# The opening of a one-core decoder step: dt in four column groups, smaller first pieces, half the zeros, and unit 2's casts in the hand-written list

## The chip, the cores and the metric

The kernel runs on one core of one Trainium2 chip. The metric is the time of one execution on the device in microseconds (us); lower is better. Engines are named as in the profile: PE (TensorE, matmul), PEld (its weight loads), DVE (VectorE), ACT (ScalarE), POOL (GpSimd) and SP (SyncE, which issues most transfers).

## The reference

One layer of a hybrid decoder for 256 prompt tokens and 8 single sample tokens, all in float32. What the change touches is its beginning: the RMSNorm and the input projection, of which dt is the last 32 columns.

```python
def rms_norm(x, g):
    xf = x.astype(jnp.float32)
    y = xf * lax.rsqrt(jnp.mean(xf * xf, axis=-1, keepdims=True) + EPS)
    return (y * g.astype(jnp.float32)).astype(x.dtype)
...
    proj = rms_norm(x, w['g_mix']) @ w['w_in']
    q, k, v, z, xbc, dt_raw = jnp.split(proj, IN_SPLITS, axis=-1)
...
    dt = jax.nn.softplus(dt_raw.astype(jnp.float32) + dt_bias.astype(jnp.float32))
```

After it come sliding-window attention, the state-space scan, an output projection, cross-attention and a convolutional feed-forward part, each with a residual. The change leaves them as they are.

## The kernel before

The tokens of both groups lie side by side as 264 columns; features lie on partitions, so x is 16 blocks `k` of 128x264 (`xT`, four tiles of four blocks). Nearly all products are float32 in three steps (`mm3`, L97 to L100): an operand is split into a rounded part `hi` in the format fp32r and a remainder `lo`, and hi·hi + hi·lo + lo·hi is accumulated. ScalarE makes `hi` (a cast of weights, or a scaling of x by the gain), VectorE makes `lo` (a subtraction).

Weights come in *units* of 8 blocks x 256 columns (128x2048), each as two *parts* of 128x1024; a part is loaded into `wraw` and split into `whi` and `wlo`. Each of these tiles has four buffers (`WBUFS`), taken in turn: the cast of part n must wait until TensorE has read part n-4. Units 0 and 1 (parts 1 to 4) give the first 256 columns of the projection, units 2 and 3 (parts 5 to 8) the next 256, unit 4 begins the third 256. The normalisation is applied at the end: r0 = 1/rms is computed beside the products, and every result is multiplied by r0 as it leaves its PSUM bank. PSUM banks go by tags: `mm` has three, `t` two, `x` and `y` one each. dt holds one `mm` bank, units 2 and 3 the two others; unit 4 takes the bank of dt when that has been evacuated.

The opening (L183 to L243) is a list written out by hand, in which SP, PE, ACT and DVE keep the order of the code. In it:

- eight F32 products of zeros (`warm`, L187) run ahead of the first data;
- x comes in pieces of two blocks (`load_x`), unit 0 in four pieces of 512 columns (`w_load`); the splits of x (`x_hi` L147, `x_lo` L151) alternate with those of the weights;
- the dt weights (128x512 for all 16 blocks) are split as well, and dt is computed in three steps per block (`dt_k`, 48 products of 32x264 through `mm3`): eight blocks between units 0 and 1, eight behind unit 1.

Behind the list a scheduler orders the work by simulated times. The norm's four squares (L305, ScalarE, each over one `xT` tile) and their sum (L306 to L309, VectorE) are held back by `issue_after`, which sets an edge from each instruction of the block to a named one *on the same engine*: here the last split of x on ScalarE and on VectorE. The sum is added over partitions by a product with ones (`total`, L274, F32), then ScalarE takes the square root (L261, with an ACT_TABLE_LOAD) and VectorE the reciprocal (L262). L328 multiplies dt by r0 and frees its bank. L405 adds the bias later.

Of the kernel before, what the change touches and what calls it, by code (L numbers as in the profile page):

```python
# [39 lines left out]
NPC = _cols()  # L40


C_ID, C_ONE, C_BLK, C_TRI, C_HM, C_MASK, C_M4 = 0, 128, 256, 384, 512, 640, 896
NCST = 900


@with_exitstack
def hybrid_decoder_step_kernel(ctx: ExitStack, tc: tile.TileContext, I, O):
    nc = tc.nc
    V, S, P, PE = nc.vector, nc.scalar, nc.gpsimd, nc.tensor  # L50

# [11 lines left out]
    def T3(pool, n, dt=F32, tag=None, name=None, bufs=None):  # L63
        return pool.tile([128, n, T], dt, tag=tag, name=name or tag, bufs=bufs)


    NPART, WBUFS = 1024, 4

    def raw_part(n=NPART):
        return wpool.tile([128, n], F32, tag="wraw", name="wraw", bufs=4)  # L70

    def weights(src, n=2048, into=None):

        out = []
        with tc.high_priority():
            for o in range(0, n, NPART):
                w = min(NPART, n - o)
                x = raw_part(w)
                nc.sync.dma_start(out=x, in_=src[:, o:o + w])
                if into:  # L80
                    hi, lo = into
                else:
                    hi = wpool.tile([128, w], F32R, tag="whi", name="whi", bufs=WBUFS)
                    lo = wpool.tile([128, w], F32R, tag="wlo", name="wlo", bufs=WBUFS)
                S.copy(out=hi, in_=x)  # L85
                V.tensor_tensor(out=lo, in0=x, in1=hi.bitcast(F32), op=ALU.subtract)  # L86
                out.append((hi, lo))
        return out
# [38 lines left out]
    xT = quarters("xT")  # L127
    par = cpool.tile([128, NPC], F32, name="par")
    cst = cpool.tile([128, NCST], F32, name="cst")
    hcol = cpool.tile([32, 2], F32, name="hcol")  # L130
    w2 = T3(apool, 8, F32R, "C", "w2").rearrange("p a t -> p (a t)")
    w_in = I["w_in"]
    small = ctx.enter_context(tc.tile_pool(name="small", bufs=2))
    A = []
    for h in range(2):
        A.append((T3(apool, 8, F32R, "A", f"xh{h}", 4), T3(apool, 8, F32R, "A", f"xl{h}", 4)))

    def load_x(j):

        nc.sync.dma_start(out=xT[j // 2][:, 2 * (j % 2):2 * (j % 2) + 2, :], in_=I["xT"][:, 2 * j:2 * j + 2, :])  # L140

    def x_of(k):
        return xT[k // 4][:, k % 4, :], par[:, k:k + 1]
# [1 line left out]
    def x_hi(k):  # L145
        x, g = x_of(k)
        return S.activation(out=A[k // 8][0][:, k % 8, :], in_=x, func=AF.Copy, scale=g)  # L147

    def x_lo(k):
        x, g = x_of(k)  # L150
        return V.scalar_tensor_tensor(out=A[k // 8][1][:, k % 8, :], in0=x, scalar=g, in1=A[k // 8][0][:, k % 8, :].bitcast(F32),  # L151
                                      op0=ALU.mult, op1=ALU.subtract)


    wraw0 = [raw_part() for _ in range(2)]
    pre = [tuple(wpool.tile([128, NPART], F32R, tag=t, name=t, bufs=WBUFS) for t in ("whi", "wlo")) for _ in range(2)]

    def w_piece(q):
        cs = slice(512 * (q % 2), 512 * (q % 2) + 512)
        return wraw0[q // 2][:, cs], pre[q // 2][0][:, cs], pre[q // 2][1][:, cs]  # L160

    def w_load(q, on):
        on.dma_start(out=w_piece(q)[0], in_=w_in[0][:, 512 * q:512 * q + 512])

    def w_hi(q):
        raw, hi, _ = w_piece(q)
        S.copy(out=hi, in_=raw)

    def w_lo(q):
        raw, hi, lo = w_piece(q)  # L170
        V.tensor_tensor(out=lo, in0=raw, in1=hi.bitcast(F32), op=ALU.subtract)


    acc0 = small.tile([128, T], F32, tag="acc", bufs=1, name="acc0")
# [3 lines left out]
    warm = psum("x")  # L178
    with tc.manual_schedule(engines={mybir.EngineType.SP, mybir.EngineType.PE, mybir.EngineType.Activation, mybir.EngineType.DVE}):
        V.memset(acc0, 0.0)  # L180
        load_x(0)
        S.dma_start(out=par[:, 0:16], in_=I["par"][:, 0:16])
        w_load(0, S)  # L183

        S.activation(out=table, in_=acc0[:, 0:1], func=AF.Copy)
        for _ in range(8):
            PE.matmul(warm[:, :T], acc0[:, 0:128], acc0, start=True, stop=True)  # L187
        for q in range(1, 4):
            w_load(q, nc.sync)
            load_x(q)  # L190
        x_hi(0)
        raw, hi, _ = w_piece(0)
        V.tensor_copy(out=hi, in_=raw)
        x_hi(1)
        x_lo(0)
        w_lo(0)
        x_lo(1)
        for q in range(1, 4):
            w_hi(q)
            w_lo(q)  # L200
            for k in (2 * q, 2 * q + 1):
                x_hi(k)
                x_lo(k)
        dthi, dtlo = (w.rearrange("p (k c) -> p k c", c=32) for w in weights(I["w_dt"].rearrange("p k c -> p (k c)"), 512, (w2[:, 0:512], w2[:, 512:1024]))[0])
        for h in range(2):
            raw = raw_part()
            nc.sync.dma_start(out=raw, in_=w_in[1][:, 1024 * h:1024 * h + 1024])
            hi, lo = (wpool.tile([128, NPART], F32R, tag=t, name=t, bufs=WBUFS) for t in ("whi", "wlo"))
            for j in (4 + 2 * h, 5 + 2 * h):
                load_x(j)  # L210
            S.copy(out=hi, in_=raw)
            V.tensor_tensor(out=lo, in0=raw, in1=hi.bitcast(F32), op=ALU.subtract)
            pre.append((hi, lo))
            for k in range(8 + 4 * h, 12 + 4 * h):
                xsplit = x_hi(k), x_lo(k)
        nc.sync.dma_start(out=cst, in_=I["cst"])
        nc.sync.dma_start(out=par[:, 16:], in_=I["par"][:, 16:])
        nc.sync.dma_start(out=hcol, in_=I["hcol"])

        def first_k(k):  # L220
            wh, wl = (w.rearrange("p (k c) -> p k c", c=256)[:, k % 4, :] for w in pre[k // 4])
            xh, xl = (a[:, k % 8, :] for a in A[k // 8])

            for i, (w, x) in enumerate(((wh, xh), (wh, xl), (wl, xh))):
                for m in range(2):
                    PE.matmul(first[m][:, :T], w[:, m * 128:(m + 1) * 128], x, start=k + i == 0, stop=k == KB - 1 and i == 2)  # L226

        def dt_k(k):
            mm3(dt_ps[0:32, :T], dthi[:, k, :], dtlo[:, k, :], A[k // 8][0][:, k % 8, :], A[k // 8][1][:, k % 8, :],
                k == 0, k == KB - 1)  # L230


        for k in range(8):
            first_k(k)
        for k in range(8):
            dt_k(k)
        for k in range(8, KB):
            first_k(k)
        for k in range(8, KB):
# [59 lines left out]


    sw = [T3(apool, 8, tag="B", name=f"sw{i}", bufs=4) for i in range(2)]
    with tc.issue_after(xsplit[0].ins), tc.issue_after(xsplit[1].ins):
        for i in range(2):
            for j in range(2):
                S.activation(out=sw[i][:, 4 * j:4 * j + 4, :], in_=xT[2 * i + j], func=AF.Square)  # L305
            V.tensor_tensor(out=sw[i][:, 0:4, :], in0=sw[i][:, 0:4, :], in1=sw[i][:, 4:8, :], op=ALU.add)  # L306
# [18 lines left out]

    dtr = t32("dtr")
    with tc.high_priority():
        V.tensor_tensor(out=dtr, in0=dt_ps[0:32, :T], in1=r0[0:32, :], op=ALU.mult)  # L328
    pair = [0]

    def in_pair(evac):
        i = pair[0]
        pair[0] += 1

        if i:
            proj([w_in[2 * i], w_in[2 * i + 1]], A, evac, tag="t" if i > 13 and i % 2 else "mm")
# [62 lines left out]
    p = psum("y")  # L399
# [5 lines left out]
    V.tensor_scalar(out=dtr, in0=dtr, scalar1=hcol[:, 0:1], scalar2=None, op0=ALU.add)  # L405
# [905 lines left out]

# [123 lines left out]
```

## Time and profile before

| what | value |
|---|---|
| median of 3 runs | 1420.21 us (1420.08 to 1420.94) |
| the profiled execution | 1417.36 us |
| its span | 1415.6 us |
| PE busy | 1404.7 us (99%) |
| DVE busy | 1047.4 us (74%) |
| ACT busy | 767.4 us (54%) |

The span runs from the first to the last instruction of the one execution that the profiler recorded; that execution's own time lies 1.8 us above its span, and the median of the runs without a profiler 2.85 us above the profiled one. A busy PE says that products stand in its queue one behind the other; their records overlap, so the distance from one start to the next is what a product costs.

### The profile page before, as it was taken

How to read it: one execution, taken by the hardware profiler on the slowest of the kernel's cores; microseconds unless marked ns; L12 is line 12 of the kernel's file. 1: busy time of each engine (PE TensorE's matmuls, PEld its weight loads, DVE VectorE, ACT ScalarE, POOL GpSimd, SP SyncE). 2: the span in 40 equal slices, each digit the busy share in tenths (PEclk: the TensorE clock that was granted, in tenths of full speed). 3: DMA queues.
4: the chain of work that ended last, by engine and by line, in shares of the span. 5: the costliest groups of instructions: out<-in, count | busy, mean ns of one | idle time of the engine just before them, and what ended most of it. 6: DMA issues, size and time to landing. Idle time of an engine off the chain costs nothing.

```text
span 1415.6 us, 29115 instructions
## 1 busy us (share of the span) xinstructions
PE 1404.7 (99%) x11561; PEld 1375.8 (97%) x11561; DVE 1047.4 (74%) x1906; ACT 767.4 (54%) x1257; POOL 91.8 (6%) x277
## 2 busy tenths in 40 slices
PE   9999999999999999999999999999999999999999
PEld 9998899999999999899999999999999999999998
DVE  7859879999996875468677775777577757765664
ACT  6557765547645555557555553555355535543432
POOL 0000001211000000020010010001000100000000
PEclk9999999999999999999999999999999999999999
DMA  8863347777766557765566675666566655555554
GB/s 289 288 194 124 128 153 253 237 230 246 249 220 243 180 190 259 259 237 192 184 227 240 223 244 183 207 234 235 181 213 226 214 180 195 197 177 190 182 190 138
DMA packets 90487, 298.32 MB, mean 211 GB/s; under 512 B 12272, under 2 KB 17264, under 8 KB 89840
## 3 DMA queue, kind: packets, MB, share of 16 engines
q1 hardware_dynamic: 84560, 277.33, 57.5%
q0 software_dynamic: 5504, 18.88, 4.1%
q8 instruction: 90, 1.47, 0.4%
q14 instruction: 45, 0.37, 0.1%
q10 hardware_dynamic: 288, 0.27, 0.1%
HBM read 280.76 MB, written 16.23 MB: 210 GB/s over the span
## 4 chain that ended last, share of the span: by engine, by line
PE 94%; DVE 3%; ACT 1%; DMA 1%; issue 1%; ACTq 0%; DVEq 0%
PE mm L98 20%; PE mm L99 20%; PE mm L100 20%; PE t L98 9%; PE t L100 9%; PE t L99 9%; DVE wlo L86 1%; PE t L226 1%; PE s L493 1%; PE t L257 1%; ACT whi L85 1%; PE t L522 1%; PE y L713 0%; PE x L187 0%; DMA wraw<-in_w_in_dram 0%
## 5 line engine op out<-in xcount | busy, mean ns | idle before, releaser
L85 ACT CAST whi<-wraw 128x1024 fp32r<-128x1024 f32 x444 | 464.1, 1048 | 536.2 <-PE mm L99 289.6
L86 DVE TENSOR_TENSOR wlo<-wraw,whi 128x1024 fp32r<-128x1024 f32 x444 | 542.8, 1224 | 250.3 <-ACT whi L85 244.3
L98 PE MATMUL t<-x2h,whi 128*128 128x264 f32 x704 | 199.9, 284 | 0.0
L98 PE MATMUL mm<-x2h,whi 128*128 128x264 f32 x704 | 199.8, 284 | 0.0
L99 PE MATMUL t<-x2l,whi 128*128 128x264 f32 x704 | 199.8, 284 | 0.0
L99 PE MATMUL mm<-x2l,whi 128*128 128x264 f32 x704 | 199.6, 284 | 0.0
L100 PE MATMUL t<-x2h,wlo 128*128 128x264 f32 x704 | 199.5, 284 | 0.0
L100 PE MATMUL mm<-x2h,wlo 128*128 128x264 f32 x704 | 199.4, 283 | 0.0
L99 PE MATMUL mm<-hl,whi 128*128 128x264 f32 x704 | 198.7, 283 | 0.0
L100 PE MATMUL mm<-hh,wlo 128*128 128x264 f32 x704 | 198.2, 283 | 0.0
L98 PE MATMUL mm<-hh,whi 128*128 128x264 f32 x704 | 197.2, 284 | 0.0
L98 PE MATMUL mm<-xh,whi 128*128 128x264 f32 x608 | 175.5, 290 | 2.7 <-DVE t L328 1.8
L100 PE MATMUL mm<-xh,wlo 128*128 128x264 f32 x608 | 174.0, 290 | 0.4 <-DVE wlo L86 0.3
L99 PE MATMUL mm<-xl,whi 128*128 128x264 f32 x608 | 174.0, 287 | 0.0
L99 PEld LDWEIGHTS t<-x2l,whi 128*128 128x128 f32 x704 | 132.6, 188 | 0.0
L99 PEld LDWEIGHTS mm<-x2l,whi 128*128 128x128 f32 x704 | 132.5, 188 | 0.0
L99 PEld LDWEIGHTS mm<-hl,whi 128*128 128x128 f32 x704 | 132.5, 188 | 0.0
L98 PEld LDWEIGHTS mm<-x2h,whi 128*128 128x128 f32 x704 | 132.5, 188 | 0.0
L98 PEld LDWEIGHTS t<-x2h,whi 128*128 128x128 f32 x704 | 132.4, 188 | 0.0
L100 PEld LDWEIGHTS t<-x2h,wlo 128*128 128x128 f32 x704 | 132.2, 188 | 0.0
L100 PEld LDWEIGHTS mm<-x2h,wlo 128*128 128x128 f32 x704 | 132.1, 188 | 0.0
L100 PEld LDWEIGHTS mm<-hh,wlo 128*128 128x128 f32 x704 | 131.9, 188 | 0.0
(460 smaller groups left out, 2936.1 us busy)
## 6 DMA issues: line engine op xcount, KB each, us to landing
wraw<-in_w_up_dram SPq DMA_DIRECT2D x176, 512.0 KB, 3.9
wraw<-in_w_in_dram SPq DMA_DIRECT2D x102, 512.0 KB, 4.4
wraw<-in_w_dn_dram SPq DMA_DIRECT2D x88, 512.0 KB, 3.9
wraw<-in_w_out_dram SPq DMA_DIRECT2D x48, 512.0 KB, 4.3
h<-in_h_dram POOLq DMA_DIRECT2D x32, 256.0 KB, 4.5
hn<-in_h_dram SPq DMA_DIRECT2D x16, 512.0 KB, 5.0
out_state_s_dram<-hn POOLq DMA_DIRECT2D x16, 512.0 KB, 3.3
e<-dram_la SPq DMA_DIRECT2D x16, 256.0 KB, 5.1
```

The costliest lines, as they stand in the source:

```text
L85: S.copy(out=hi, in_=x)
L86: V.tensor_tensor(out=lo, in0=x, in1=hi.bitcast(F32), op=ALU.subtract)
L98: PE.matmul(out, wh, xh, start=start, stop=False)
L99: PE.matmul(out, wh, xl, start=False, stop=False)
L100: PE.matmul(out, wl, xh, start=False, stop=stop)
L226: PE.matmul(first[m][:, :T], w[:, m * 128:(m + 1) * 128], x, start=k + i == 0, stop=k == KB - 1 and i == 2)
L257: PE.transpose(out, in_, cst[0:k, C_ID:C_ID + k])
L493: PE.matmul(s3, qT[:, j, c * 128:c * 128 + 128], kbd[:, pp, :, 0:nk], start=True, stop=True)
L522: PE.matmul(o[64 * h:64 * h + 64, 0:128], vn[:, kb, pp, 64 * h:64 * h + 64], pt[:, h * nb + kb, :], start=kb == 0, stop=kb == nb - 1)
```

## The change

- **Pieces.** The first two pieces of x and of unit 0 are one block each; the later ones of unit 0 two. The list has x ahead of the weights where it was the other way round. Unit 1 comes in its two parts as before.
- **Zeros.** Four in place of eight.
- **dt.** Its weights are no longer split: they come as F32 behind all of x (`wdt`), VectorE multiplies them by the gain once, and dt is computed from the raw x in 16 F32 products behind unit 1, four rounds of four; product j of a round writes partitions 32j to 32j+31. The four partial sums are multiplied by r0 together (`dt4`, 128x264), and one more F32 product with a matrix of zeros and ones (`C_SUM`) adds them; the addition of the bias reads its result.
- **Casts.** Unit 2's loads and splits are in the list now, behind those of unit 1. The edge of the squares' block is on the last of them on VectorE (`wlast`), and on nothing on ScalarE.

```diff
-        for _ in range(8):
+        for _ in range(4):
             PE.matmul(warm[:, :T], acc0[:, 0:128], acc0, start=True, stop=True)
...
+        for k in (2, 4, 6):
+            load_x(k, 2)
+            w_load(k, 2)
+        for k in (0, 1):
+            x_hi(k)
+            raw, hi, _ = w_piece(k, 1)
+            V.tensor_copy(out=hi, in_=raw)
+            x_lo(k)
+            w_lo(k, 1)
+        for k in (2, 4, 6):
+            x_hi(k)
+            w_hi(k, 2)
+            x_hi(k + 1)
+            x_lo(k)
+            w_lo(k, 2)
+            x_lo(k + 1)
+        w_load(8, 4)
...
+        nc.sync.dma_start(out=wdt, in_=I["w_dt"])
+        for k in (8, 12):
+            x_hi(k)
+            w_hi(k, 4)
+            for i in range(1, 4):
+                x_hi(k + i)
+            x_lo(k)
+            w_lo(k, 4)
+            for i in range(1, 4):
+                x_lo(k + i)
+        V.tensor_tensor(out=wdt, in0=wdt, in1=par[:, 0:16].unsqueeze(2).broadcast_to([128, KB, 32]), op=ALU.mult)
+
+        for k in (16, 20):
+            w_load(k, 4)
+            w_hi(k, 4)
+            wlast = w_lo(k, 4)
...
+        def dt_round(r):
+
+            for j in range(4):
+                k = 4 * r + j
+                PE.matmul(dt_ps[32 * j:32 * j + 32, :T], wdt[:, k, :], xT[k // 4][:, k % 4, :], start=r == 0, stop=r == 3)
+
+        for k in range(KB):
             first_k(k)
-        for k in range(8):
-            dt_k(k)
-        for k in range(8, KB):
-            first_k(k)
-        for k in range(8, KB):
-            dt_k(k)
+        for r in range(4):
+            dt_round(r)
...
-    with tc.issue_after(xsplit[0].ins), tc.issue_after(xsplit[1].ins):
+    with tc.issue_after(wlast.ins):
         for i in range(2):
             for j in range(2):
                 S.activation(out=sw[i][:, 4 * j:4 * j + 4, :], in_=xT[2 * i + j], func=AF.Square)
...
-        V.tensor_tensor(out=dtr, in0=dt_ps[0:32, :T], in1=r0[0:32, :], op=ALU.mult)
+        dt4 = small.tile([128, T], F32, tag="raw", name="dt4")
+        V.tensor_tensor(out=dt4, in0=dt_ps[:, :T], in1=r0, op=ALU.mult)
+
+    dt_sum = psum("x")
+    PE.matmul(dt_sum[0:32, :T], cst[:, C_SUM:C_SUM + 32], dt4, start=True, stop=True)
+    V.tensor_scalar(out=dtr, in0=dt_sum[0:32, :T], scalar1=hcol[:, 0:1], scalar2=None, op0=ALU.add)
```

Where instructions stand, first on ScalarE from the weights of blocks 4 and 5 on to the end of the squares; `xh` are the splits of x, `sw` the squares, `whi` and `w` weight casts. Before:

```order
L147 ACTIVATE xh_78<-xT_68,par 128x264 x2
L167 CAST whi<-wraw 128x512
L147 ACTIVATE xh_78<-xT_68,par 128x264 x2
L85 CAST w_74<-wraw 128x512
L211 CAST whi<-wraw 128x1024
L147 ACTIVATE xh_80<-xT_69,par 128x264 x4
L211 CAST whi<-wraw 128x1024
L147 ACTIVATE xh_80<-xT_70,par 128x264 x4
L305 ACTIVATE sw_332<-xT_67 128x1056
L305 ACTIVATE sw_332<-xT_68 128x1056
L305 ACTIVATE sw_333<-xT_69 128x1056
L305 ACTIVATE sw_333<-xT_70 128x1056
```

After:

```order
L320 ACTIVATE sw_310<-xT_68 128x1056
L172 CAST whi<-wraw 128x512
L146 ACTIVATE xh_78<-xT_68,par 128x264
L146 ACTIVATE xh_80<-xT_69,par 128x264
L172 CAST whi<-wraw 128x1024
L146 ACTIVATE xh_80<-xT_69,par 128x264 x3
L320 ACTIVATE sw_311<-xT_69 128x1056
L146 ACTIVATE xh_80<-xT_70,par 128x264
L172 CAST whi<-wraw 128x1024
L146 ACTIVATE xh_80<-xT_70,par 128x264 x3
L320 ACTIVATE sw_311<-xT_70 128x1056
L172 CAST whi<-wraw 128x1024 x2
```

Each square now stands behind the first splits that read its tile, among the splits, and unit 2's two casts stand behind the last square; the first square (not shown) stands behind the split of block 2.

On ScalarE, from there to the square root `r` with its table load. Before:

```order
L429 ACTIVATE abc<-par 128x32
L85 CAST whi<-wraw 128x1024
L426 ACTIVATE acol<-hcol 32x1
L85 CAST whi<-wraw 128x1024 x6
L261 ACT_TABLE_LOAD
L261 ACTIVATE r_345<-y,eps 128x264
L85 CAST whi<-wraw 128x1024
```

After:

```order
L172 CAST whi<-wraw 128x1024 x2
L448 ACTIVATE abc<-par 128x32
L445 ACTIVATE acol<-hcol 32x1
L85 CAST whi<-wraw 128x1024 x6
L276 ACT_TABLE_LOAD
L276 ACTIVATE r_323<-y,eps 128x264
```

Seven casts stood between the squares and the root (parts 5 to 11), now eight do (parts 5 to 12).

On TensorE, at the end of unit 3 (`xh_80`, `xl_81`) and the beginning of unit 4 (`xh_78`, `xl_79`). Before, the total (L274) stood inside unit 3, 19 products from its end; the end itself:

```order
L98 MATMUL mm<-xh_80,whi 128x264
L99 MATMUL mm<-xl_81,whi 128x264
L100 MATMUL mm<-xh_80,wlo 128x264
L98 MATMUL mm<-xh_78,whi 128x264
L99 MATMUL mm<-xl_79,whi 128x264
```

After:

```order
L98 MATMUL mm<-xh_80,whi 128x264
L99 MATMUL mm<-xl_81,whi 128x264
L100 MATMUL mm<-xh_80,wlo 128x264
L289 MATMUL y<-acc_82,cst 128x264
L347 MATMUL x<-dt_335,cst 32x264
L98 MATMUL mm<-xh_78,whi 128x264
L99 MATMUL mm<-xl_79,whi 128x264
```

The total (now L289) stands behind unit 3, and the summing product of dt (L347) between it and unit 4.

## Rows read from the trace of the kernel before

**Rows 1.** The page, its head and the first line of its part 1: busy time, share of the span and instructions of TensorE.

```profile
span 1415.6 us, 29115 instructions
...
PE 1404.7 (99%) x11561; PEld 1375.8 (97%) x11561; DVE 1047.4 (74%) x1906; ACT 767.4 (54%) x1257; POOL 91.8 (6%) x277
```

**Rows 2.** The waits of TensorE over the whole span: who waited, for whom, us in total, times, longest.

```profile
PE mm L98 <- DVE t L328: 1.8, 1, 1.8
...
PE mm L99 <- DVE ohl L1095: 0.9, 1, 0.9
PE mm L98 <- ACT whi L85: 0.8, 1, 0.8
```

**Rows 3.** TensorE's timeline, 0 to 40 us: start, time, line and operation, tiles, count, and in brackets idle time and who ended it.

```profile
1.20 6.42 PE L187 MATMUL x<-acc 128*128 128x264 f32 x16 [1.20 <-DVE eps L253]
7.26 0.60 PE L226 MATMUL t<-xh,whi 128*128 128x264 f32 x2
...
13.28 0.28 PE L98 MATMUL mm<-xh,w 128*32 128x264 f32 x1
...
16.18 0.40 PE L226 MATMUL t<-xh,whi 128*128 128x264 f32 x2
...
22.00 0.28 PE L98 MATMUL mm<-xh,w 128*32 128x264 f32 x1
...
24.90 0.28 PE L98 MATMUL mm<-xh,whi 128*128 128x264 f32 x1
...
34.20 0.61 PE L274 MATMUL y<-acc,cst 128*128 128x264 f32 x2
...
34.77 0.29 PE L98 MATMUL mm<-xh,whi 128*128 128x264 f32 x1
...
36.84 0.28 PE L100 MATMUL mm<-xh,wlo 128*128 128x264 f32 x1
38.96 0.36 PE L98 MATMUL mm<-xh,whi 128*128 128x264 f32 x1 [1.83 <-DVE t L328]
```

**Rows 4.** TensorE's timeline in two short stretches within the zeros; each row begins with the first record of its stretch. An F32 product has two records.

```profile
4.44 1.53 PE L187 MATMUL x<-acc 128*128 128x264 f32 x3
...
4.88 1.53 PE L187 MATMUL x<-acc 128*128 128x264 f32 x3
```

**Rows 5.** ScalarE's timeline, 3 to 37 us.

```profile
3.68 0.92 ACT L147 ACTIVATE xh<-xT,par 128x264 fp32r<-128x264 f32 x2 [0.52 <-DMA par<-in_par_dram]
4.92 0.62 ACT L167 CAST whi<-wraw 128x512 fp32r<-128x512 f32 x1 [0.32 <-DMA wraw<-in_w_in_dram]
6.59 0.92 ACT L147 ACTIVATE xh<-xT,par 128x264 fp32r<-128x264 f32 x2 [1.06 <-DMA xT<-in_xT_dram]
7.75 0.63 ACT L167 CAST whi<-wraw 128x512 fp32r<-128x512 f32 x1 [0.23 <-DMA wraw<-in_w_in_dram]
8.65 0.93 ACT L147 ACTIVATE xh<-xT,par 128x264 fp32r<-128x264 f32 x2 [0.27 <-DMA xT<-in_xT_dram]
9.48 0.60 ACT L167 CAST whi<-wraw 128x512 fp32r<-128x512 f32 x1
10.00 0.92 ACT L147 ACTIVATE xh<-xT,par 128x264 fp32r<-128x264 f32 x2
...
11.90 1.05 ACT L211 CAST whi<-wraw 128x1024 fp32r<-128x1024 f32 x1 [0.47 <-DMA wraw<-in_w_in_dram]
12.86 1.73 ACT L147 ACTIVATE xh<-xT,par 128x264 fp32r<-128x264 f32 x4
...
17.13 4.00 ACT L305 ACTIVATE sw<-xT 128x1056 f32<-128x1056 f32 x4
...
33.68 1.05 ACT L85 CAST whi<-wraw 128x1024 fp32r<-128x1024 f32 x1 [1.84 <-PE mm L99]
34.75 1.28 ACT L261 ACT_TABLE_LOAD   x1
36.04 0.48 ACT L261 ACTIVATE r<-y,eps 128x264 f32<-128x264 f32 x1
```

**Rows 6.** VectorE's timeline, 5 to 39 us.

```profile
5.17 0.43 DVE L193 CAST whi<-wraw 128x512 fp32r<-128x512 f32 x1 [4.02 <-DMA wraw<-in_w_in_dram]
...
15.75 1.22 DVE L212 TENSOR_TENSOR wlo<-wraw,whi 128x1024 fp32r<-128x1024 f32 x1
...
36.55 1.80 DVE L262 RECIPROCAL r<-r 128x264 f32<-128x264 f32 x1 [0.57 <-ACT r L261]
38.39 0.42 DVE L328 TENSOR_TENSOR t<-mm,r 32x264 f32<-32x264 f32 x1
38.74 0.41 DVE L369 TENSOR_TENSOR raw<-t,r 128x264 f32<-128x264 f32 x1
```

**Rows 7.** TensorE's timeline around L574, later in the program: sixteen F32 products of 129 columns in four rounds of four column groups, two records each, and the product behind them.

```profile
196.50 1.09 PE L574 MATMUL s<-kcT,zz 128*32 128x129 f32 x32
197.51 0.39 PE L99 MATMUL mm<-xl,whi 128*128 128x264 f32 x1
```

**Rows 8.** TensorE's timeline behind its longest wait in the middle of the program.

```profile
403.18 0.39 PE L98 MATMUL t<-ath,whi 128*128 128x264 f32 x1 [2.02 <-DVE u L778]
403.41 0.28 PE L99 MATMUL t<-atl,whi 128*128 128x264 f32 x1
403.53 0.28 PE L100 MATMUL t<-ath,wlo 128*128 128x264 f32 x1
```

More of the change, by code (lines that the diff above doesn't have):

```diff
@@ L40 @@
 NPC = _cols()
-C_ID, C_ONE, C_BLK, C_TRI, C_HM, C_MASK, C_M4 = 0, 128, 256, 384, 512, 640, 896
-NCST = 900
+C_ID, C_ONE, C_BLK, C_TRI, C_HM, C_MASK, C_M4, C_SUM = 0, 128, 256, 384, 512, 640, 896, 900
+NCST = 932
 @with_exitstack
@@ L130, in hybrid_decoder_step_kernel @@
     hcol = cpool.tile([32, 2], F32, name="hcol")
-    w2 = T3(apool, 8, F32R, "C", "w2").rearrange("p a t -> p (a t)")
+    wdt = T3(apool, 8, F32, "C", "wdt").rearrange("p a t -> p (a t)")[:, 0:512].rearrange("p (k c) -> p k c", c=32)
     w_in = I["w_in"]
@@ L136, in hybrid_decoder_step_kernel, with load_x @@
         A.append((T3(apool, 8, F32R, "A", f"xh{h}", 4), T3(apool, 8, F32R, "A", f"xl{h}", 4)))
-    def load_x(j):
-        nc.sync.dma_start(out=xT[j // 2][:, 2 * (j % 2):2 * (j % 2) + 2, :], in_=I["xT"][:, 2 * j:2 * j + 2, :])
+    def load_x(k, n):
+        nc.sync.dma_start(out=xT[k // 4][:, k % 4:k % 4 + n, :], in_=I["xT"][:, k:k + n, :])
     def x_of(k):
@@ L152, in x_lo, with unit_part, w_load, w_piece @@
                                       op0=ALU.mult, op1=ALU.subtract)
[L155 to L166, printed above, removed]
+    def unit_part(o=None):
+        raw = raw_part()
+        return (raw, *(wpool.tile([128, NPART], F32R, tag=t, name=t, bufs=WBUFS) for t in ("whi", "wlo")))
+    pre = []
+    def w_load(k, n, on=nc.sync):
+        if k % 4 == 0:
+            pre.append(unit_part())
+        c = 256 * (k % 4)
+        on.dma_start(out=pre[k // 4][0][:, c:c + 256 * n], in_=w_in[k // 8][:, 256 * (k % 8):256 * (k % 8 + n)])
+    def w_piece(k, n):
+        return (w[:, 256 * (k % 4):256 * (k % 4 + n)] for w in pre[k // 4])
+    def w_hi(k, n):
+        raw, hi, _ = w_piece(k, n)
         S.copy(out=hi, in_=raw)
-    def w_lo(q):
-        raw, hi, lo = w_piece(q)
-        V.tensor_tensor(out=lo, in0=raw, in1=hi.bitcast(F32), op=ALU.subtract)
+    def w_lo(k, n):
+        raw, hi, lo = w_piece(k, n)
+        return V.tensor_tensor(out=lo, in0=raw, in1=hi.bitcast(F32), op=ALU.subtract)
     acc0 = small.tile([128, T], F32, tag="acc", bufs=1, name="acc0")
@@ L180, in hybrid_decoder_step_kernel @@
         V.memset(acc0, 0.0)
-        load_x(0)
+        load_x(0, 1)
         S.dma_start(out=par[:, 0:16], in_=I["par"][:, 0:16])
-        w_load(0, S)
+        w_load(0, 1, S)
+        load_x(1, 1)
+        w_load(1, 1, S)
         S.activation(out=table, in_=acc0[:, 0:1], func=AF.Copy)
-        for _ in range(8):
+        for _ in range(4):
             PE.matmul(warm[:, :T], acc0[:, 0:128], acc0, start=True, stop=True)
-        for q in range(1, 4):
-            w_load(q, nc.sync)
-            load_x(q)
@@ L191, in hybrid_decoder_step_kernel @@
[L191 to L215, printed above, removed]
+        for k in (2, 4, 6):
+            load_x(k, 2)
+            w_load(k, 2)
@@ new lines, in hybrid_decoder_step_kernel @@
+        for k in (0, 1):
[12 more added lines that the diff above has]
+        w_load(8, 4)
+        load_x(8, 2)
+        load_x(10, 2)
+        w_load(12, 4)
+        load_x(12, 2)
+        load_x(14, 2)
+        nc.sync.dma_start(out=wdt, in_=I["w_dt"])
@@ L220, in first_k @@
         def first_k(k):
-            wh, wl = (w.rearrange("p (k c) -> p k c", c=256)[:, k % 4, :] for w in pre[k // 4])
+            wh, wl = (w.rearrange("p (k c) -> p k c", c=256)[:, k % 4, :] for w in pre[k // 4][1:])
             xh, xl = (a[:, k % 8, :] for a in A[k // 8])
@@ L226, in first_k @@
                     PE.matmul(first[m][:, :T], w[:, m * 128:(m + 1) * 128], x, start=k + i == 0, stop=k == KB - 1 and i == 2)
-        def dt_k(k):
-            mm3(dt_ps[0:32, :T], dthi[:, k, :], dtlo[:, k, :], A[k // 8][0][:, k % 8, :], A[k // 8][1][:, k % 8, :],
-                k == 0, k == KB - 1)
-        for k in range(8):
-            first_k(k)
-        for k in range(8):
-            dt_k(k)
-        for k in range(8, KB):
-            first_k(k)
-        for k in range(8, KB):
-            dt_k(k)
+        def dt_round(r):
[3 more added lines that the diff above has]
+        for k in range(KB):
+            first_k(k)
+        for r in range(4):
+            dt_round(r)
+    pre2 = [p[1:] for p in pre[4:]]
     def pc(name, i=0, n=1):
@@ L335, in in_pair @@
         if i:
-            proj([w_in[2 * i], w_in[2 * i + 1]], A, evac, tag="t" if i > 13 and i % 2 else "mm")
+            proj([pre2 if i == 1 else w_in[2 * i], w_in[2 * i + 1]], A, evac, tag="t" if i > 13 and i % 2 else "mm")
         else:
@@ L403, in hybrid_decoder_step_kernel @@
     S.copy(out=vn.rearrange("p a b c -> p (a b c)"), in_=p)
-    V.tensor_scalar(out=dtr, in0=dtr, scalar1=hcol[:, 0:1], scalar2=None, op0=ALU.add)
     ea = t32("ea")
@@ L1308, in _consts @@
     c[:, C_MASK + 128:C_MASK + 256] = np.where(i[None, :] <= i[:, None], 0.0, NEG)
+    c[:, C_SUM:C_SUM + 32] = i[:, None] % 32 == np.arange(32)[None, :]
     c[:, C_M4:C_M4 + 4] = i[:, None] % 4 == np.arange(4)[None, :]
```

## The prediction

> **What bounds the kernel now.** I read the page's first lines, then TensorE's waits, then the timelines of the first 40 us engine by engine. TensorE is busy 1404.7 us of a span of 1415.6 [rows 1], so the change is worth what TensorE works or waits less. Of the waits that the profile names, one lies in the stretch that is changed: 1.8 us until L328, the evacuation of dt [rows 2]. In the timeline TensorE runs the zeros from 1.20, the first product of a real block at 7.26, dt's two halves at 13.28 and 22.00, unit 2 from 24.90, and goes on without idle time to the last product of unit 3 at 36.84, which is over at 36.96; it resumes at 38.96 with unit 4 [rows 3]. The banks explain that wait: unit 4 takes the bank of dt, which is free when dt has been multiplied by r0. So 38.96 is set by the chain to r0: a weight cast on ScalarE at 33.68, a table load at 34.75, the square root at 36.04, the reciprocal on VectorE at 36.55, the evacuation at 38.39 [rows 5, 6]. That the cast is ahead of the root is the program's order; the cast itself waits for TensorE to let go of a weight buffer. After 38.96 TensorE is the bound again, so the change is worth what it does to the moment at which unit 4 starts.
>
> **Zeros and first pieces.** The halves of the zeros' F32 products start 0.44 us apart [rows 4], so one takes 0.88 and four end at 1.20 + 3.5 = 4.7 in place of 7.24. What block 0 needs is there at about that time: ScalarE began its first split at 3.68 and VectorE its first weight cast at 5.17 [rows 5, 6], which now waits for a piece of half the size. TensorE can start 2.5 us earlier.
>
> **dt.** Before: 24 products from 13.28 to 16.18 and 24 from 22.00 to 24.90 [rows 3], 5.8 us. After: 16 F32 products of 264 columns in four rounds of four column groups. A lone F32 product of 264 columns takes 0.45 (L274 at 34.20, one other product of 0.12, and 34.77) [rows 3]; of 129 columns it would be 0.22, and sixteen 3.5. The sixteen column-group products of L574, two records each, fill about 1.0, from 196.50 to 197.51 [rows 7]. So four groups run side by side, and dt takes 16 x 0.45 x 1.0/3.5 = 2.05. Gain 3.75. On VectorE the new product of dt's weights with the gain takes the place of the old subtraction of the same size.
>
> **What feeds TensorE.** Were that all, unit 3 would end 6.2 us earlier. It won't: before, every split was ready in time because the zeros and dt's first half kept TensorE busy meanwhile. And in the new order of ScalarE the four squares are not behind unit 2's casts: the edge is on a VectorE instruction and holds VectorE's additions alone. Three squares come ahead of the last weight cast for blocks 12 to 15. ScalarE's work from the split of block 2 to that cast: 11 splits at 0.415 (two take 0.83, from 8.65 to 9.48), 3 casts of 512 at 0.52 (9.48 to 10.00), 2 of 1024 at 0.96 (11.90 to 12.86), 3 squares at 0.98 (four take 4.00 with the last one's tail) [rows 5]: 4.6 + 1.6 + 1.9 + 2.9 = 11.0. Blocks 2 and 3 are complete when 0.8 MB have been asked for, as much as had landed when the cast at 4.92 began [rows 5]; I take 5.2. Without further waits the cast ends at 16.2. Before, ScalarE waited 1.06 + 0.23 + 0.27 + 0.47 for landings after that one [rows 5]; the squares fill part of such waits, so I take 0.8 of these 2.0: 17.0, with ends of 16.2 and 17.6. VectorE's subtraction, 1.22 [rows 6]: 18.2. Then TensorE has 20 products of blocks 12 to 15 left at 0.121 (units 2 and 3 are 96, 11.6 of the 12.06 from 24.90 to 36.96, the total is the rest), 2.4: 20.6; dt 2.05: 22.7; units 2 and 3 11.6: **34.3 against 36.96** (ends 33.5 and 34.9). Of the 6.2 us, 2.7 are left. Unit 2's own casts follow the last square, at about 18.2, and end by 20.5, in time.
>
> **The chain to r0.** Here the change costs. Before, seven weight casts stand between the squares and the root, those of parts 5 to 11; after, those of parts 5 to 12 do. Weight buffers go in turns of four: part 11 takes that of part 7, which TensorE lets go three quarters through units 2 and 3 (36.96 - 2.9 - 0.45 = 33.6; the cast starts at 33.68), and part 12 that of part 8, which it lets go at their end, 34.3. From the start of that last cast to TensorE's restart it took 38.96 - 33.68 = 5.28: cast 1.05, table 1.28, root 0.48, reciprocal 1.80, evacuation 0.42, and what lies between [rows 5, 6]. Evacuating 128 partitions in place of 32 adds nothing: L369's 128x264 took 0.41 [rows 6]. After: 34.35 + 5.28 = 39.6. And what stands behind the total in TensorE's queue is not unit 4 but the new summing product, which waits for that evacuation, with all of unit 4 queued behind it. It takes 0.45, as a lone F32 product does [rows 3]: **unit 4 starts at 40.1 against 38.96, 1.1 later.** TensorE's idle time there grows from 2.0 to 4.9. So: 2.7 won up to unit 3's end, 0.45 given back as the total moves from inside unit 3 behind it, 2.9 more of waiting, 0.45 for the sum. With the ends of the feed: 0.4 to 1.7 later.
>
> **Behind it.** The chain from dt to its transposes starts some 1 us later too, and up to about 110 us the scheduler has moved a few instructions; TensorE may wait there where it does not now. I take 0.3, between nothing and 0.8, the size of one of its small waits elsewhere [rows 2]. Later TensorE's order is the one it was.
>
> **Sum.** 1.1 + 0.3 = +1.4 us: a span of 1417.0 after 1415.6, an execution of 1418.8 after the profiled one's 1417.36. The runs' median, 1420.21, lies 2.85 above that execution, a part that the change doesn't touch, so the median becomes **1421.6**. A measurement of this kernel tells about 0.2%, 2.8 us, from no change, so this is no change.
>
> **TensorE's clock.** Of its two levels, 1.2 and 2.4 GHz, the zeros show the lower: halves 0.44 apart [rows 4], where a half of L274 is 0.225 [rows 3]. After the idle 2.0 us at 403 the products are 0.12 apart at once [rows 8], so a gap of that length cost no speed; one of 4.9 is not in the trace.
> The Trainium skill, TensorE: Matmul & The Clock Gate (HAM oscillation), says that long gaps while TensorE waits for data bring the lower level back, so that the next work starts cold; no row here shows that, and by it the sum would be the first rival's.
>
> **The rivals.**
> - *The clock falls in the gap* (slower). Unit 4 then starts at the lower level. The price: the eight zeros took 6.04 us, and eight lone F32 products take 3.6, so 2.4 lost. 1.4 + 2.4 = +3.8: 1424.0. It decides if 4.9 us of idleness are enough where 2.0 were not. For it: TensorE began at the lower level after standing idle. Against: the wait at 403 only. Chance 0.25.
> - *The gate does not bind*: r0 is ready when unit 3 ends. Unit 4 then starts at 34.3 plus two F32 products, 35.2, which is 3.8 earlier; with 0.3 behind it 1416.7, faster by 0.25%. For it: the squares are done on ScalarE by 19, so the sum under the root is there in time. Against: cast, table, root and reciprocal stand in program order behind unit 3's end. Chance 0.04.
> - *Column groups take turns*: dt takes 16 x 0.45 = 7.2, 5.1 more, 1426.7. L574 speaks against it. Chance 0.03.
>
> **How the numbers follow.** My forecast has 0.68, between 1420.5 (no waits in the feed, nothing behind) and 1422.7. To hold eight in ten the range must reach into the clock's case, and I leave some room below for pieces that land sooner: 1419.8 to 1424.3. Slower by over 0.2% is above 1423.0: 0.03 of the groups and 0.21 of the clock, whose cold stretch may be shorter than the start's, 0.24. Faster is 0.04, and within 0.2% the rest, 0.72.
>
> **What would show it.** Right: ScalarE busy throughout from about 5 to 19 us with squares among its splits, and small idle stretches of TensorE there; dt in about 2 us; unit 3's end near 34.3; one wait of near 5 us ended by dt's evacuation, and the restart near 39.6. Wrong: a root that runs before 35, dt's records one behind the other, products 0.24 apart after the wait, or unit 3's end before 33 or after 35.5.

## The result, and the profile after

| | median | runs |
|---|---|---|
| before | 1419.41 us (1416.91 to 1421.18) | 20 |
| after | 1422.76 us (1420.62 to 1425.23) | 20 |

The ratio is 1.0025 (95% interval 1.0019 to 1.0031): the medians are 3.3 us apart, where the forecast had 1.4. The median of before is that of twenty executions; the forecast started from three, 1420.21. The profiled execution took 1421.45 us with a span of 1419.7, 4.1 us more than before's [rows 1].

TensorE's timeline of the kernel after, the opening:

```profile
1.20 3.50 PE L194 MATMUL x<-acc 128*128 128x264 f32 x8 [1.20 <-DVE eps L268]
5.12 0.48 PE L243 MATMUL t<-xh,whi 128*128 128x264 f32 x2 [0.43 <-ACT xh L146]
...
14.79 0.51 PE L243 MATMUL t<-xh,wlo 128*128 128x264 f32 x2 [0.52 <-DVE wlo L176]
...
20.95 1.99 PE L249 MATMUL mm<-xT,wdt 128*32 128x264 f32 x32
22.87 0.39 PE L98 MATMUL mm<-xh,whi 128*128 128x264 f32 x1
```

The first real product starts at 5.12 in place of 7.26, small waits for the feed follow, dt takes 1.92 us, and unit 2 starts at 22.87 in place of 24.90 [rows 3]. Up to here the change wins 2.0 us. The same view, from the end of unit 3 on:

```profile
34.65 0.61 PE L289 MATMUL y<-acc,cst 128*128 128x264 f32 x2
40.02 1.06 PE L347 MATMUL x<-dt,cst 128*32 128x264 f32 x2 [4.76 <-DVE dt L344]
41.00 0.59 PE L98 MATMUL mm<-xh,whi 128*128 128x264 f32 x1
41.39 0.42 PE L99 MATMUL mm<-xl,whi 128*128 128x264 f32 x1
41.61 0.42 PE L100 MATMUL mm<-xh,wlo 128*128 128x264 f32 x1
...
45.13 0.29 PE L98 MATMUL mm<-xh,whi 128*128 128x264 f32 x1
45.26 0.29 PE L99 MATMUL mm<-xl,whi 128*128 128x264 f32 x1
```

Read the distances of the starts: behind the wait of 4.76 the products stand 0.22 apart until 45.13, then 0.12. The windows view of the stretch, with TensorE's busy time and records, the granted clock as a share of 2.4 GHz, the share of the DMA engines and GB/s:

```profile
4.20:38.30 34.10, 29.05 (x229) 1.00 0.87 310
38.30:45.13 6.83, 5.11 (x20) 0.50 0.79 277
45.13:60.00 14.87, 14.87 (x121) 1.00 0.69 238
```

From 38.30, within the wait, to 45.13 the granted clock is 0.50, 1.2 GHz. The same columns for the kernel before, its wait before unit 4 [rows 3] included:

```profile
36.00:46.00 10.00, 8.17 (x65) 1.00 0.83 277
```

What released the wait is in ScalarE's timeline and, its last two rows, VectorE's:

```profile
18.16 1.07 ACT L320 ACTIVATE sw<-xT 128x1056 f32<-128x1056 f32 x1
...
34.73 1.04 ACT L85 CAST whi<-wraw 128x1024 fp32r<-128x1024 f32 x1 [1.88 <-PE mm L99]
35.79 1.28 ACT L276 ACT_TABLE_LOAD   x1
37.09 0.48 ACT L276 ACTIVATE r<-y,eps 128x264 f32<-128x264 f32 x1
```

```profile
37.60 1.80 DVE L277 RECIPROCAL r<-r 128x264 f32<-128x264 f32 x1 [0.57 <-ACT r L276]
39.44 0.43 DVE L344 TENSOR_TENSOR dt<-mm,r 128x264 f32<-128x264 f32 x1
```

ScalarE worked off the squares among the splits, as forecast, and is done with them at 19.2; yet the root waits until part 12's cast has run, and that cast until unit 3 has ended: 34.73, 5.29 before the summing product at 40.02 ([rows 5, 6] show the same chain before). Unit 4 starts at 41.00, 2.04 later than before. Its first 18 products take 4.13 us, up to 45.13; in e1, below, where the clock stays at 1.00, the same 18 take 2.27 (40.69 to 42.96): 1.86 lost. The sum is 3.90. The reciprocal of the attention's norm on VectorE, before and after:

```profile
97.70 0.35 DVE L262 RECIPROCAL rqs<-rqs 128x32 f32<-128x32 f32 x1 [0.38 <-ACT rqs L261]
101.66 0.35 DVE L277 RECIPROCAL rqs<-rqs 128x32 f32<-128x32 f32 x1 [0.38 <-ACT rqs L276]
```

It is 3.96 later, so nearly all of the loss is made by 45 us.

**The clock in the other executions.** Each result lists an execution's mean granted clock. All 20 executions of the kernel after lie below 1.000 (0.996 to 0.999). Of 89 executions of the kernel before beside the experiments, 25 have 1.000 (median 1417.95 us), 34 have 0.999 (1418.8) and 30 have 0.998 (1420.0); one with 0.948 is left out. The profile of before, 1417.36 us, was of the first kind. This mean says nothing of the program's first microseconds: while the zeros run the granted clock reads 1.00 in every profile, although their halves are 0.44 apart [rows 4].

### The profile page after: what moved, and what is told of

It is laid out like the page before. It is cut to its first block, busy times and chain, and to the rows that moved or that the text cites. A ratio compares the mean times of both kernels' runs of the same rounds, so it can differ in the third digit from the quotient of the medians.

```text
span 1419.7 us, 29074 instructions
## 1 busy us (share of the span) xinstructions
PE 1404.0 (99%) x11539; PEld 1371.9 (97%) x11539; DVE 1049.2 (74%) x1908; ACT 767.4 (54%) x1256; POOL 91.3 (6%) x277
## 4 chain that ended last, share of the span: by engine, by line
PE 94%; DVE 3%; DMA 2%; ACT 1%; issue 1%; ACTq 0%; DVEq 0%
PE mm L98 20%; PE mm L99 20%; PE mm L100 20%; PE t L98 9%; PE t L100 9%; PE t L99 9%; DVE wlo L86 1%; PE s L512 1%; PE t L272 1%; PE t L541 1%; PE y L732 0%; DMA out_conv_new_dram<-cnew 0%; DMA xT<-in_xT_dram 0%; DMA h<-in_h_dram 0%; PE y L748 0%
```

## The experiments

The theory: the opening gains some 2 us up to unit 3's end and loses them because the root stands behind part 12's cast, so that TensorE waits 4.8 us before unit 4; in that wait the clock falls, which costs 2.3 us more. All ratios are against the kernel before on the same chip; "at 1.000" counts executions with that mean clock.

| run | ratio (95% interval) | median us | at 1.000 |
|---|---|---|---|
| e1, wait filled | 1.0001 (0.9992 to 1.0010) | 1419.96 | 8 of 11 |
| e2, root first | 0.9988 (0.9979 to 0.9997) | 1417.71 | 4 of 11 |
| e3, eight zeros | 1.0015 (1.0006 to 1.0024) | 1421.41 | 0 of 11 |
| e4, columns alone | 0.9985 (0.9977 to 0.9994) | 1417.62 | 9 of 11 |
| e5, squares last | 1.0026 (1.0016 to 1.0036) | 1422.34 | 0 of 8 |
| e6, other banks | 0.9991 (0.9982 to 0.9999) | 1416.85 | 4 of 11 |
| e7, before with other banks | 0.9986 (0.9977 to 0.9994) | 1416.65 | 4 of 11 |
| e8, other banks, squares last | 0.9978 (0.9969 to 0.9987) | 1415.58 | 5 of 11 |
| e9, before, wait at 403 filled | 0.9991 (0.9982 to 1.0000) | 1417.87 | 3 of 11 |
| e10, before, wait at 37 filled | 0.9994 (0.9985 to 1.0003) | 1418.11 | 9 of 11 |
| e11, before, both filled | 0.9992 (0.9984 to 1.0001) | 1418.22 | 11 of 11 |
| e12, e8 with the wait at 403 filled | 0.9967 (0.9954 to 0.9979) | 1414.85 | 5 of 5 |

The medians of before were 1419.32 beside e1 to e4, 1418.54 beside e5 to e8, 1419.20 beside e9 to e12.

**e1: is the clock a cost of its own?** The total is written out, `tot` being its product.

```diff
...
+    busy = psum("x")
+    with tc.issue_after(tot.ins):
+        for _ in range(9):
+            PE.matmul(busy[:, :T], ones, acc0, start=True, stop=True)
```

> Nine spare F32 products of 264 columns stand behind the total on TensorE, into a bank that is free, and fill some 4.1 of the 4.8 us that it waits for dt's evacuation; the chain to r0 is not touched. They add work whose result nobody reads. If the lower clock behind the wait is a cost of its own: the granted clock stays at 1.0 through the wait, the summing product takes 0.45 in place of 0.98 and unit 4's products stand 0.12 apart from the first, so that about 2.3 us of the changed kernel's 3.3 over before are gone: 1420.4 where before is 1419.4, a ratio of 1.0007. Rival, the late chain alone costs: the products change nothing, 1.0025 again.

TensorE's timeline of e1, then its window of the stretch (columns: busy time and records of PE, PEld, DVE, ACT, POOL, clock, DMA share, GB/s):

```profile
34.78 0.61 PE L326 MATMUL y<-acc,cst 128*128 128x264 f32 x2
35.23 4.17 PE L332 MATMUL x<-acc,cst 128*128 128x264 f32 x18
40.15 0.60 PE L354 MATMUL x<-dt,cst 128*32 128x264 f32 x2 [0.76 <-DVE dt L351]
40.69 0.39 PE L98 MATMUL mm<-xh,whi 128*128 128x264 f32 x1
...
42.96 0.28 PE L98 MATMUL mm<-xh,whi 128*128 128x264 f32 x1
```

```profile
38.30:46.00 7.70, 6.94 (x48) 5.85 (x48) 5.77 (x12) 5.10 (x9) 0.00 (x0) 1.00 0.75 261
```

The chain is where it was (40.15 for 40.02), the clock stays at 1.00, the sum takes 0.54 in place of 0.98, and the reciprocal that was at 101.66 comes at 99.44: 2.2 us back for work that nobody reads. The ratio of 1.0025 is outside the interval; the rival falls. The median is even level with before, since many executions of before pay for their own wait there (e10).

**e2: is the order cast, table, root the cause of the long wait?** `root` is the square root's instruction, `evac_dt` that of L344, `tot` the total's product; `cast` reaches the splits of both parts of unit 5, 11 and 12, as `behind`; through `last` the final twelve products of unit 3 stand behind the total.

```diff
-                S.copy(out=hi, in_=x)
-                V.tensor_tensor(out=lo, in0=x, in1=hi.bitcast(F32), op=ALU.subtract)
+                with ExitStack() as held:
+                    for b in behind or ():
+                        held.enter_context(tc.issue_after(b.ins))
+                    S.copy(out=hi, in_=x)
+                    V.tensor_tensor(out=lo, in0=x, in1=hi.bitcast(F32), op=ALU.subtract)
...
+                        with tc.issue_after(last.ins) if last and ui == 1 and pi == 1 and m >= 1 else ExitStack():
+                            mm3(outs[m][:, :n], wh[:, k, m * 128:(m + 1) * 128], wl[:, k, m * 128:(m + 1) * 128],
...
+                 cast=(root, evac_dt) if i == 2 else None, last=tot if i == 1 else None)
```

> The eighth weight cast (part 12) is held behind the root on ScalarE and its subtraction behind dt's evacuation on VectorE, and the last 12 products of unit 3 behind the total. If the order cast, table, root behind unit 3's end is what made the wait long: the root runs near 33.5, TensorE's wait before the summing product shrinks from 4.8 to 1.6 to 2.2 us, the clock stays at its upper level and unit 4 starts at 37.3 (36.7 to 37.6) in place of 41.0: 1.7 us below before and 5 below the changed kernel, a ratio of 0.9988. Rival, the root is late for another reason (the sum under it, the table): it runs at 36 or later all the same and the time is that of the changed kernel, 1.0025. Second rival, part 12 is now late and unit 5 waits for it: unit 4 starts early, and the gain is given back some 12 us later.

Rows of e2, ScalarE and then TensorE:

```profile
30.50 1.28 ACT L332 ACT_TABLE_LOAD   x1
34.37 0.48 ACT L332 ACTIVATE r<-y,eps 128x264 f32<-128x264 f32 x1 [2.59 <-PE y L330]
34.75 2.00 ACT L88 CAST whi<-wraw 128x1024 fp32r<-128x1024 f32 x2
```

```profile
33.72 0.61 PE L330 MATMUL y<-acc,cst 128*128 128x264 f32 x2
...
37.30 0.60 PE L355 MATMUL x<-dt,cst 128*32 128x264 f32 x2 [1.52 <-DVE dt L352]
37.84 0.39 PE L101 MATMUL mm<-xh,whi 128*128 128x264 f32 x1
```

The table load is out of the chain and the casts stand behind the root. The wait shrinks to 1.52 and unit 4 starts at 37.84, 3.2 earlier than in the changed kernel (0.5 of the forecast is missing since this run's opening was fed 0.5 later: unit 2 at 23.42). The ratio is the expected 0.9988. Cast, table and root behind unit 3's end are thus what makes the wait, but the edit changes two things. Here the root starts 0.65 behind the total's start; in the changed kernel it could by this estimate have run at 34.65 + 0.65 = 35.30, and ran at 37.09. So the order of cast, table and root is worth 1.8 of the 3.24 us by which the wait shrinks. The other 1.45 are, as an estimate, the total's move ahead of twelve products of 0.121. The two were not run apart.

**e3 and e5: zeros and squares.** e3 has `range(8)` again. e5:

```diff
-            w_hi(k, 4)
+            wcast = w_hi(k, 4)
             wlast = w_lo(k, 4)
...
-    with tc.issue_after(wlast.ins):
+    with tc.issue_after(wlast.ins), tc.issue_after(wcast.ins):
```

> The changed kernel with eight zeros again; TensorE is held up to 8.0 us by them in place of 4.7. If what feeds TensorE set the end of unit 1: the late start is made up while later splits are waited for, unit 3 ends within 0.3 us of 34.65 and the time is that of the changed kernel, 1.0025 of before (1.0023 to 1.0030). Rival, the halved zeros carry 2.5 us: unit 3 ends near 37 and the time is 2 us more, 1.004.

> The changed kernel with the norm's squares held behind unit 2's last cast on ScalarE too, not only the additions on VectorE. If the squares among the splits delay what feeds TensorE: unit 3 ends 0.7 us earlier (34.0 in place of 34.65), but the cast of part 12, the table load and the root still follow unit 3's end, so that the wait stays at 4.7 us and the clock falls in it again; unit 4 starts at 40.3 in place of 41.0: 1.0020 of before (1.0013 to 1.0026). Rival, the squares were the main loss and with them gone the wait closes: 1.000 or less.

TensorE's timeline of e3:

```profile
1.20 5.61 PE L194 MATMUL x<-acc 128*128 128x264 f32 x16 [1.20 <-DVE eps L268]
6.45 0.60 PE L243 MATMUL t<-xh,whi 128*128 128x264 f32 x2
...
34.96 0.61 PE L289 MATMUL y<-acc,cst 128*128 128x264 f32 x2
```

The first real product starts 1.33 later than after, not up to 8.0 us as expected, since the zeros took only 5.61 us in this execution; the total at unit 3's end comes 0.3 later. So 0.3 of these 1.33 us stay. The ratio excludes the rival's 1.004; it also lies below the forecast's range (1.0023 to 1.0030), though its interval overlaps that of the changed kernel. In e5 unit 3 ends 0.5 earlier, but the wait is 4.76 again, and the time does not move. TensorE's timeline of e5, and a window (TensorE's columns as above):

```profile
5.57 0.47 PE L243 MATMUL t<-xh,whi 128*128 128x264 f32 x2 [0.74 <-ACT xh L146]
...
7.38 0.48 PE L243 MATMUL t<-xh,whi 128*128 128x264 f32 x2 [0.65 <-ACT xh L146]
7.70 0.69 PE L243 MATMUL t<-xl,whi 128*128 128x264 f32 x2
...
39.49 1.06 PE L347 MATMUL x<-dt,cst 128*32 128x264 f32 x2 [4.76 <-DVE dt L344]
```

```profile
7.00:9.00 2.00, 1.62 (x8) 0.71 1.01 369
```

In this execution the clock falls near 7.8 us and stays down until 11.3, behind two short waits for splits, 0.74 and 0.65; in e8's profile, with a wait of 0.94 at the same place, it is 1.00 from 5 to 12. What made the difference was not found. What the squares' order is worth is seen only without the long wait (e8).

**e4: dt in column groups alone**, in the kernel before; the edit is the diff's part on dt, with the loads, zeros and squares of before.

> The kernel before with dt alone changed: four column groups, F32, and the summing product; eight zeros, the old pieces and the old order of the squares. If the eighth cast ahead of the root is an effect of the other edits: unit 3 ends 1.8 to 2.4 us earlier than before, the wait behind it stays near 2 us, the clock stays up and unit 4 starts at 37.5 (37.2 to 38.0) in place of 38.96: 1.4 us below before, a ratio of 0.9990. Rival, the summing product or F32 columns bring the long wait themselves: a wait of 4 us or more, a lower clock behind it, 1.001 or more.

TensorE's timeline of e4:

```profile
37.81 0.60 PE L330 MATMUL x<-dt,cst 128*32 128x264 f32 x2 [1.82 <-DVE dt L327]
```

The wait before the sum is 1.82 and the clock stays up in this profile: the columns do not bring the long wait. Unit 4 starts at 38.34, later than forecast, because TensorE now waits twice 0.74 for `xl` in blocks 8 to 15, where dt's first half had covered that. At equal clock little is won: its executions at 1.000 have a median of 1417.62, those of before 1417.95. The rest of the ratio goes with fewer executions that lose the clock, 2 of 11. Why they are so few, with waits of 1.82 and 2.02 left, was not shown.

**e6 to e8: nothing of unit 4 waits for r0.** e6 is the changed kernel with other banks, e7 the kernel before with the same edit, e8 has e5's edit as well.

```diff
-    dt_ps = psum("mm")
+    dt_ps = psum("x")
...
-    warm = psum("x")
+    warm = psum("mm")
...
-            proj([pre2 if i == 1 else w_in[2 * i], w_in[2 * i + 1]], A, evac, tag="t" if i > 13 and i % 2 else "mm")
+            proj([pre2 if i == 1 else w_in[2 * i], w_in[2 * i + 1]], A, evac, tag=["mm", "s"] if i == 2 else "t" if i > 13 and i % 2 else "mm")
```

The bank `pq`, the first use of `s` before, is asked for behind units 4 and 5.

> The changed kernel with dt in the bank that the zeros used, the zeros in one of the three banks of the projections, and units 4 and 5 in the third of these and in the attention's bank, which is unused until then; the order behind it is the scheduler's. Nothing that unit 4 needs now waits for r0. If the bank of dt alone ties unit 4 to the chain: TensorE has no wait between unit 3 and unit 4, unit 4 starts at 34.4 (34.0 to 34.8), the total and the summing product (0.9 and 0.45) run among its products, the clock stays up, and the time is 3.3 us below before and 6.5 below the changed kernel: 1416.1 where before is 1419.4, a ratio of 0.9977. Rival, something else holds unit 4 or 5 there (part 12's cast, the weights' transfers, the evacuations of units 2 and 3 that still wait for r0): a wait of 2 us or more within the next 20 us, and 0.999 or more.

> The same change of banks in the kernel before, its opening untouched. If the 2.0 us before unit 4 are only the bank: they go, unit 4 follows unit 3 at 37.0, and the time is 2.0 us below before: a ratio of 0.9986 (0.9980 to 0.9992). Rival, TensorE then waits for the weights instead: 1.000. Beside the run before this one it tells what the opening is worth once the chain to r0 binds in neither: 1.3 us by the sum (2.3 at unit 3's end, less 0.45 for the total, which the kernel before has inside unit 3's time already, and 0.45 for the sum).

> Both the other banks and the squares behind unit 2's casts, in the changed kernel. If the two effects add: unit 3 ends at 34.0, unit 4 follows at once, and the time is 4.0 us below before: 1415.4, a ratio of 0.9972 (0.9965 to 0.9980). Rival, the squares done later make the total late and TensorE waits for it or for r0 further on: 0.998 or more.

In all three TensorE goes from unit 3 to unit 4 without a wait. Unit 4 starts at 35.16 in e6 (0.8 later than forecast; the feed was 0.5 later in that run) and at 36.68 in e7. e7 comes out as expected. e6 misses its forecast: at the reciprocal it is 2.6 us ahead of before (95.09 against 97.70), and the span ends only 0.7 longer than before's. Two things took 2.8 of these 3.3 us. Waits of 0.77 before 219.97 and of 0.28 and 0.73 near 298, for VectorE, stand where before has 0.23 and 0.28. And at 403 TensorE's timeline of e6 shows this, with a window of all engines:

```profile
402.26 0.39 PE L98 MATMUL t<-ath,whi 128*128 128x264 f32 x1 [2.02 <-DVE u L798]
...
403.15 0.42 PE L98 MATMUL t<-ath,whi 128*128 128x264 f32 x1
403.37 0.42 PE L99 MATMUL t<-atl,whi 128*128 128x264 f32 x1
...
406.44 0.28 PE L98 MATMUL t<-ath,whi 128*128 128x264 f32 x1
```

```profile
402.30:406.00 3.70, 3.70 (x19) 3.70 (x20) 3.70 (x7) 2.25 (x6) 0.00 (x0) 0.59 0.68 198
```

The wait is the one of [rows 8], 2.02 us, but here the clock falls behind it, until 406.4, and 1.5 us are lost. e6 against e7 also says what the opening is worth where the chain to r0 binds in neither: nothing that can be measured (0.9991 and 0.9986; forecast 1.3 us). At the reciprocal e6 is 0.2 ahead of e7 (95.09 and 95.30). With the squares behind unit 2's casts (e8) the ratio is 0.9978 and the reciprocal comes at 94.18, 0.9 ahead of e6: there the order of the squares shows, though the intervals of e6 and e8 overlap.

**e9 to e12: the waits of 2 us.** `spare` puts four products behind a given one: behind unit 3's last in e10 and e11, and in e9, e11 and e12 behind the last of the second group of output-projection products, ahead of the group that waits at 403. Nobody reads their results.

```diff
+    def spare(after, tag, n):
+        busy = psum(tag)
+        with tc.issue_after(after.ins):
+            for _ in range(n):
+                p = PE.matmul(busy[:, :T], ones, cst[:, 0:T], start=True, stop=True)
+        return p
...
+            if i == 1:
+                spare(last, "x", 4)
...
+        ends.append(proj([w_out[i]], [AT], ev, tag="t" if i % 2 else "mm",
+                         after=spare(ends[1], "s", 4) if i == 3 else None))
```

> The kernel before with four spare F32 products (work that nobody reads) in TensorE's 2.0 us wait at 403, nothing else. In the profile of e6 the clock was at its lower level from 403 to 406 behind that wait, in the profile of before it was not; and of 62 executions of before the mean granted clock was 1.000 in 19 (median 1417.95 us), 0.999 in 24 (1418.72), 0.998 in 19 (1420.12). If a wait of 2 us lowers the clock in a part of the executions: with this one covered, fewer executions are below 1.000, none for this wait, and the median is 0.4 to 1.0 us lower, a ratio of 0.9993 to 0.9997. Rival, the scatter has other causes (the transfers): the same share of executions below 1.000, and a ratio of 1.000.

> The kernel before with four spare F32 products in TensorE's wait before unit 4, at 37 to 39, nothing else. By the same theory: the executions at 0.998 vanish or become few, those at 0.999 (the wait at 403) stay; the median falls by 0.5 to 1.2 us, a ratio of 0.9992 to 0.9996. Rival: no change, 1.000.

> The kernel before with both waits covered. By the theory: the mean clock is 1.000 in all executions, they scatter less, and the median is that of the executions of before with 1.000, some 1.0 us below before's median: a ratio of 0.9992 (0.9988 to 0.9996). Rival: 1.000, with clocks of 0.998 and 0.999 as before.

> The kernel of e8 (the other banks, the squares behind unit 2's casts) with the wait at 403 covered by four spare products. By the theory: the mean clock is 1.000 in all executions; the median is that of the executions of e8 with 1.000, 1414.7 where before is 1418.5: a ratio of 0.9973 (0.9965 to 0.9980). Rival, the cover does nothing: 0.9978 and clocks of 0.999 in half of the executions.

The windows of e9 and of e10 (all engines), each in the wait that it leaves open:

```profile
39.00:46.00 7.00, 6.48 (x38) 6.33 (x39) 5.82 (x14) 4.62 (x7) 0.00 (x0) 0.76 0.95 334
```

```profile
403.50:409.00 5.50, 4.73 (x26) 4.73 (x27) 5.50 (x13) 2.25 (x6) 0.00 (x0) 0.69 0.70 221
```

In e9 the clock falls behind the wait at 37 (2.32 in this execution), in e10 behind that at 403 (2.08). The profile of e1 shows the latter too, first TensorE's timeline, then a window of all engines:

```profile
405.54 0.59 PE L98 MATMUL t<-ath,whi 128*128 128x264 f32 x1 [2.02 <-DVE u L804]
```

```profile
405.50:409.00 3.50, 3.46 (x15) 3.46 (x16) 3.50 (x6) 2.25 (x6) 0.00 (x0) 0.51 0.63 194
```

e9 by itself is inconclusive: the share below 1.000 did not shrink. e10 misses a part of its forecast: not only the executions at 0.998 became few but also those at 0.999, which were to stay; 2 of 11 are below 1.000. e11 is clear: with both covered all 11 executions have 1.000, where of before 64 of 89 are below, and none is above 1419.38, where before, on the same chip, goes to 1420.81; that its median is lower, by 1.0 us, has an interval that touches 1. e12 has 1.000 in all five executions and the lowest ratio of all, 0.9967 of before, 4.7 us (3.0 to 6.5) less; its interval overlaps that of e8.

## Why the prediction failed in its likeliest case

The time lies in the range, through a rival to which 0.25 was given: the clock falls in the gap. Luck has a part in how near the number is: the three executions of before that it starts from have a median 0.8 above that of all twenty, which hides that much of the miss. Step by step:

- *Zeros and first pieces.* Start 2.5 us earlier: measured 2.14. Most of it is spent in waits for the feed, as said; in e3 0.3 of 1.33 stays.
- *dt* in 2.05 us: 1.92. Right; the four column groups run side by side.
- *Feed*, unit 3's end at 34.3: 34.65, inside the bounds of 33.5 and 34.9. Two terms missed and cancelled: ScalarE's split of block 2 began at 5.80 in place of 5.2, and its waits for landings behind that were 0.15 in place of 0.8.
- *The chain to r0.* Seven casts become eight, and the last is released by unit 3's end: right. The 5.28 us from that cast to the restart were 5.29. e2 takes the chain out: with the root first, and the total ahead of twelve products, the wait is 1.52.
- *The summing product* at 0.45: it took 0.98, at the lower clock; 0.54 in e1.
- *TensorE's clock.* Here the forecast failed. The price of the rival, 2.4, came out: 0.44 in the sum and 1.86 in unit 4 are 2.3, and e1 gets 2.2 back. That was partly luck, for it was taken from the zeros of one execution, and those of e7, 1.2 us shorter, would have given 1.2. What was wrong is the step from the wait at 403 to the gap, and with it the chance. The only evidence against it was that the products are 0.12 apart behind the 2.0 us at 403 [rows 8]. That was one execution: the profiles of e1, e6 and e10 show the same wait followed by the lower clock. A gap of 2 us was no safe ground for one of 5.
- *Behind it*, 0.3: the reciprocal at 101.66 leaves 0.06.
- *The sum* was made against the profiled execution, and its distance of 2.85 to the median was called a part that the change doesn't touch. It was not: the profile of before is of an execution at 1.000, and before loses the clock itself in most executions, in its waits of about 2 us (e9 to e11). So after is 4.1 us above before between the two profiles but 3.3 between the medians: before already pays a part of what after always pays.

The Trainium skill, TensorE: Matmul & The Clock Gate (HAM oscillation), says that long gaps while TensorE waits for data bring the lower level back. The kernel after, e3 and e5, which all have the long wait, agree: none of their 39 executions is at 1.000. That gaps of 2.0 to 2.3 us do it in a part of the executions is what e6, e9 and e10 add.

## What to carry to other kernels

A product that is blocked by a bank ties TensorE to the chain that frees the bank: give the next unit a bank that is free (e6 to e8), or bring the chain's own instructions, the sum under the root included, ahead of casts that are not due (e2), before shortening what comes ahead of it. Price a wait of TensorE with the clock behind it, here 2.3 us on top of 4.8, and don't conclude from one profile that a gap is harmless: look at the mean clock of all executions. Where a wait can't be removed, a few spare products in it may pay (e1).

## What the runs showed of the hardware that was not expected

- The same wait of about 2 us is followed by the lower clock in some executions and not in others: at 403 in the profiles of e1, e6 and e10, but not in those of before, after, e2 to e5, e7 and e8. How often also differs between kernels: where the wait at 403 is the only one of this length, 2 of 11 executions of e10 lie below 1.000 and 7 of 11 of e7. What decides it was not found; that it is the waits is shown by e11, where all executions of the kernel before keep 1.000 once both are filled.
- The clock can fall when TensorE is already at work again: in e6 it resumes at 402.26 and its products are 0.22 apart from 403.15 on. After the long wait the lower level held for 5.1 us of work (40.02 to 45.13), in e6 for 3.3.
- The eight zeros, which wait for nothing in between, took 6.42 us in the profile of before [rows 3], 6.43 in e4, 5.61 in e3 and 5.22 in e7. Their halves are 0.44 apart at first and 0.22 later, and the change comes at different moments, worth up to 1.2 us in the zeros. How much of it reaches the end of an execution was not measured; in e7 unit 3 ends only 0.3 earlier than in before. The zeros of e7, which use another bank, in TensorE's timeline:

```profile
1.20 5.22 PE L187 MATMUL mm<-acc 128*128 128x264 f32 x16 [1.20 <-DVE eps L253]
```
